# Half-precision operand pairs in the down projection of both feed-forward layers

## The chip, the cores and the metric

The kernel runs on one core of a Trainium2 chip. Its engines work from queues of their own, each strictly in order: TensorE (PE; its weight loads are PEld), VectorE (DVE), ScalarE (ACT), GpSimd (POOL) and the sync engine (SP), which issues most loads. The metric is device time in microseconds for one execution: the median of several runs. One more execution is recorded by the hardware profiler.

## The reference

Two layers of a diffusion backbone run over 1024 latent tokens and 256 context tokens of width 1024. After each mixer comes a modulated SwiGLU feed-forward layer of inner width 2816:

```python
def swiglu(u, w_gate, w_up, w_down):
    return (jax.nn.silu(u @ w_gate) * (u @ w_up)) @ w_down
...
h_lat = h_lat + g2 * swiglu(modulate(rms_norm(h_lat, norm2_g[i]), sh2, sc2),
                            ffn_w_gate[i], ffn_w_up[i], ffn_w_down[i])
if not last:
    h_ctx = h_ctx + cg1 * y_ctx
    h_ctx = h_ctx + cg2 * swiglu(modulate(rms_norm(h_ctx, norm2_g[i]), csh2, csc2),
                                 ffn_w_gate[i], ffn_w_up[i], ffn_w_down[i])
```

All inputs and outputs are float32.

## The kernel before

Activations are held with features on the 128 partitions and tokens along the free axis. The inner width is 22 blocks of 128, worked on as 11 pairs (`n2`); the latent tokens are two halves of 512 columns. A pair of blocks times the two halves is a 2x2 block product, and it is done by Winograd's scheme: seven products in place of eight, each of sums and differences of the blocks.

Float32 precision comes from operand pairs: each operand is split into a high and a low part, and every product takes three matmuls (high by high, high by low, low by high). There are two kinds of split. `split` casts to F32R on ScalarE and subtracts on VectorE. `half_split` scales by a column, rounds to float16 on ScalarE, and forms the scaled rest in float16 on VectorE. Gate and up use scaled half-precision pairs, down uses F32R pairs.

**Gate and up** (`ffn`). For each pair i the weights of gate, then up, are loaded (`wino_weights`), bounded by `weight_scale` (a scale from the sum of absolute values, so that no scaled weight can overflow), and split into seven operand pairs. `wino_steps` then issues the products in steps: A11 with B11 into PSUM tile `pa`; A12 with B21 into `pc`; S1 with T1 into `pb`; then S2, S3 and A22 onto `pa`, with a copy taken between them (`snap`); last S4 with B22 onto `pb`. Each product is 12 matmuls (four blocks of the contraction by three), each of 512 columns. The steps of gate and up of pair i are mixed with the last steps of up of pair i - 1. PSUM tiles come from `PS`, by turns out of one pool of six and one of two banks (out of the six alone in layer 0 at this point). `finish(i)` multiplies the four evicted up blocks by the gate blocks (after SiLU), forms the sums and differences that down needs, and stores seven tiles to DRAM (`bops`). The gate tiles come from a pool of four. `sums(i)` loads the four blocks of pair i of the down weights, forms S1 to S4 on VectorE, and stores them to DRAM (`sops`). In layer 0, the conditioning of the next layer (`ada_group`, line 448) is computed on VectorE meanwhile.

The instructions of each engine are put in order by a scheduler at build time, which goes by dependencies, buffers and the order of the program; tiles of a pool are given out in the program's order.

**Down** (`down`). Seven products, each summed over the 11 pairs: for every pair the operand of weights and that of activations are loaded side by side into one tile of 128x1024, split, and multiplied with 12 matmuls into four PSUM tiles (three for each tile). Tiles come from a pool of 20. `evict` scales a finished block by a column of the conditioning and adds it to the residual stream. In the last product the last three pairs (layer 0) or four pairs (layer 1) are multiplied block by block at the end; in layer 1 in two halves of 256 columns. The context tokens' down in layer 0 is a separate loop at the end of `down`.

Of the kernel before, what the change touches and what calls it, by code (L numbers as in the profile page):

```python
# [10 lines left out]
F32 = mybir.dt.float32  # L11
F32R = mybir.dt.float32r
# [17 lines left out]
WID = {0: 512, 1: 512, 2: 256, 3: 256, 4: 256}  # L30
OFF = {0: 0, 1: 512, 3: 512, 4: 768}
KSTART = (0, 8, 24, 32)
PAD_C, PAD_T, SHIFT = 96, 112, 16
BOPS = ("B11", "B21", "T2", "T1", "T3", "B22", "T4")


# [165 lines left out]
class Builder:  # L202
# [970 lines left out]
        self.ucol = cols  # L1173
        self.usi = us[:, 1:2]

    def weight_scale(self, tiles):

        nc = self.nc
        n = len(tiles)
        st = self.pt.tile([P, 16], F32, tag="st", name=self.nm("st"))  # L1180
        junk = self.T(BF16, 1024)
        for k, t in enumerate(tiles):
            nc.scalar.activation(junk[:, :t.shape[1]], t, AF.Abs, scale=2.0 ** -15, accum_out=st[:, k:k + 1])
        sb = st[:, 8:9].bitcast(BF16)
        with nc.allow_low_precision(reason="a bound, within a factor of two"):
            nc.vector.tensor_reduce(sb[:, 0:1], st[:, :n], axis=AX, op=ADD)
        ps = self.PS()
        self.mm(ps[:, 0:1], self.ones.bitcast(BF16)[:, 1::2], sb[:, 0:1], True, True)
        k = 3 * len(self.wsc)
        s, b, inv = (self.wcol[:, k + j:k + j + 1] for j in range(3))  # L1190
        nc.vector.tensor_scalar(b, ps[:, 0:1], 1e-30, None, op0=MAX)
        nc.vector.reciprocal(s, b)
        nc.vector.tensor_scalar(inv, b, self.usi, None, op0=MUL)
        return s, inv
# [178 lines left out]
    def ffn(self, l, u, h, hs, second, after, keep=None, begun={}):  # L1373
# [3 lines left out]
        bops = [{k: self.DR([P, 512]) for k in BOPS} for _ in range(n2)]  # L1377
        sops = [{k: self.DR([P, 512]) for k in ("S1", "S2", "S3", "S4")} for _ in range(n2)]
        hidc = [self.DR([P, 2, 256]) for _ in range(n2 if u is not None else 0)]
        def sums(i):  # L1380

            w = a["down"][l]
            t = [self.S2() for _ in range(4)]
            a21, a22, a11, a12 = t
            with self.follow(self.last_ld):
                for x, (k, r) in zip(t, ((0, 1), (1, 1), (0, 0), (1, 0))):
                    self.ld(x, w[2 * i + k, r])
            nc.vector.tensor_tensor(a22, a21, a22, ADD)  # L1388
# [28 lines left out]
        def finish(i, gate):  # L1417

            up = self.res
            inv = self.wsc[(l, i, 1)][1]  # L1420
            for k, g in gate.items():
                nc.vector.scalar_tensor_tensor(g, up[k], inv, g, op0=MUL, op1=MUL)  # L1422
            b11, b12, b21, b22 = gate[(0, 1)], gate[(0, 0)], gate[(1, 1)], gate[(1, 0)]
            t1, t2, t4 = up[(0, 0)], up[(0, 1)], up[(1, 1)]
            nc.vector.tensor_tensor(t1, b12, b11, SUB)
# [17 lines left out]
        for i in range(n2):  # L1443
            g, up = begun.get((i, 0)), begun.get((i, 1))
            if g is None or not g.whole:
                wg = waiting.pop((i, 0))
                w = next(wg)
                next(wg)
            fetch(i, 1)
            if g is None:  # L1450
                g = Steps(self.wino_steps(w, self.G))
                g.to(1)
            if prev is not None:
                prev[0].to(7)
                finish(i - 1, prev[1])
            wu = waiting.pop((i, 1))
            w = next(wu)
            if up is None:
                up = Steps(self.wino_steps(w, self.TK))
            if i == 0:  # L1460
                for k, _ in enumerate(second):
                    if k == 11:
                        next(wu)
            next(wu, None)
            fetch(i + 1, 0)
            for k in (3, 4, 5) if i == 0 and l == 1 else ():
# [12 lines left out]
            up.to(5)  # L1479
            prev = (up, gate)  # L1480
            for k in (2 * i - 2, 2 * i - 1) if l == 1 else (9, 10) if i == 9 else (i,) if i < 9 else ():
                if 0 <= k < n2:
                    sums(k)
            for _ in range(2):
                next(todo, None)
        prev[0].to(7)
        finish(n2 - 1, prev[1])
        self.down(l, bops, sops, hidc, hs, h, todo, after, keep)

    def down(self, l, bops, sops, hidc, hs, h, todo, after, keep):
        nc, a = self.nc, self.a
        w = a["down"][l]
        n2 = NFB // 2
        self.banks = 6

        def operands(asrc, bsrc, own):
            hi, lo = self.S4(F32R), self.S4(F32R)
            f = self.S4() if own else lo.bitcast(F32)  # L1500
            self.ld(f[:, :512], asrc)
            self.ld(f[:, 512:], bsrc)
            self.split(f, hi, lo)
            return hi, lo

        def prods(acc, ops, j, c0, c1, first, last):
# [20 lines left out]
        def evict(acc, r, j, pc, final):  # L1527
            nb = 4 * r + j
            n = WID[pc]
            c0 = OFF[pc] % 512 if pc > 2 else 0  # L1530
            t = h.ap(0, nb, pc)
            nc.vector.scalar_tensor_tensor(t, acc[j][:, c0:c0 + n], self.ada_col(l, pc, 5, nb), t, op0=MUL, op1=ADD)
            if final and pc < 3:
                self.square(t, nb, pc)
                if l == 0 and pc < 2:
                    self.lda(keep[nb][:, pc * 512:pc * 512 + 512], t)
            elif final and j < 3:
                x = self.TK()
# [15 lines left out]
        for p, (ak, bk, r, pc, final) in enumerate(seq):  # L1554
            acc = sets[p % 2]
            late = []
            for i in range(n2):
# [700 lines left out]
```

## Time and profile before

| | us |
|---|---|
| runs, median of 3 (lowest to highest) | 3015.81 (3011.55 to 3017.45) |
| profiled execution, its own time | 3016.71 |
| profiled execution, span from first to last instruction | 3014.9 |
| mean granted TensorE clock | 0.982 |

The page sums up the engines' busy time over the span and lists groups of instructions by source line. These are the largest groups of matmuls; the columns after the bar are the busy time, the mean duration in ns, and the idle time of the engine before them with what ended it:

```profile
L1324 PE MATMUL ps<-s,s 128*128 128x512 f16 x2100 | 477.3, 383 | 16.5 <-DVE s L1221 8.6
L1511 PE MATMUL ps<-s,s 128*128 128x512 f32 (+1 forms) x1000 | 261.2, 384 | 9.0 <-DVE s L289 8.7
```

Line 1324 is gate and up, line 1511 is down, lines 287 and 289 are the two steps of `split`, lines 1146 and 1147 those of `half_split`, and lines 1183 to 1193 are `weight_scale`. Matmuls overlap, so that their rate is read from how many fit into a stretch, not from the duration of one. Rows of a stretch show the stretch's length, then busy time and count by engine, the granted clock (PEclk), the share of the DMA engines, and GB/s.

### The profile page before, as it was taken

The numbers are of one execution on the slowest core, as the hardware profiler recorded it, in microseconds if no ns is written. First come the engines' busy times: TensorE is split into PE (matmuls) and PEld (weight loads), VectorE is DVE, ScalarE is ACT, GpSimd is POOL, SyncE is SP. The second block draws the span as 40 slices with busy tenths as digits, with TensorE's granted clock in tenths as the row PEclk, the third lists the DMA queues.
The fourth block names the chain that finished last, engine by engine and source line by source line (L and its number), as shares of the span: only waits on it lengthen the run. The fifth ranks groups of instructions, "written<-read, shape, count | busy, mean of one in ns | idle before, by whom it ended". The sixth has DMA issues, their size and how long they took to land. (4 is left out here: it accounts for less than half of the span.)

```text
span 3014.9 us, 46087 instructions
## 1 busy us (share of the span) xinstructions
PE 2864.5 (95%) x16364; PEld 2085.2 (69%) x16364; DVE 2108.4 (70%) x4181; ACT 1511.8 (50%) x2761; POOL 530.8 (18%) x883
## 2 busy tenths in 40 slices
PE   7899999899998999999999999999999799999997
PEld 3678888888897444447778888878777344444886
DVE  5767786674677988866767437777776898765555
ACT  4663325452456555443445336777774655543433
POOL 1012013451111212131020002222231022112000
PEclk9899999999999999999999999999999899999999
DMA  7564545366555555657874344444555376424663
GB/s 256 190 202 166 176 143 173 119 189 213 200 210 196 211 187 206 221 207 270 290 245 153 126 130 119 134 137 121 180 175 192 134 275 235 149 81 165 217 192 130
DMA packets 253681, 551.47 MB, mean 183 GB/s; under 512 B 33926, under 2 KB 69448, under 8 KB 253450
## 3 DMA queue, kind: packets, MB, share of 16 engines
q1 hardware_dynamic: 191658, 357.63, 35.7%
q0 software_dynamic: 59488, 186.70, 17.5%
q10 hardware_dynamic: 2304, 4.20, 0.4%
q8 instruction: 129, 2.11, 0.3%
q14 instruction: 102, 0.84, 0.1%
HBM read 420.20 MB, written 119.80 MB: 179 GB/s over the span
## 5 line engine op out<-in xcount | busy, mean ns | idle before, releaser
L1324 PE MATMUL ps<-s,s 128*128 128x512 f16 x2100 | 477.3, 383 | 16.5 <-DVE s L1221 8.6
L1324 PEld LDWEIGHTS <-s 128*128 128x128 f16 x2640 | 259.1, 98 | 334.5 <-issue 28.4
L283 PE MATMUL ps<-s,wh 128*128 128x256 f32 (+1 forms) x1780 | 393.6, 327 | 1.5 <-ACT wh L287 1.5
L283 PEld LDWEIGHTS ps<-s,wh 128*128 128x128 f32 x1780 | 293.2, 188 | 36.5 <-ACT wh L287 3.1
L283 PE MATMUL pq<-s,wh 128*128 128x512 f32 (+1 forms) x972 | 297.4, 385 | 4.7 <-DVE s L2088 2.5
L1511 PE MATMUL ps<-s,s 128*128 128x512 f32 (+1 forms) x1000 | 261.2, 384 | 9.0 <-DVE s L289 8.7
L287 ACT CAST s<-s 128x1024 fp32r<-128x1024 f32 (+2 forms) x188 | 171.7, 942 | 180.0 <-DMA s<-d 146.9
L283 PE MATMUL ps<-s,wl 128*128 128x256 f32 (+1 forms) x890 | 257.7, 327 | 2.3 <-DVE wl L289 2.3
L283 PE MATMUL ps<-s,s 128*128 128x64 f16 (+3 forms) x2663 | 216.1, 233 | 24.0 <-DVE st L1800 9.9
L287 ACT CAST wh<-ws 128x1024 fp32r<-128x1024 f32 (+1 forms) x99 | 100.4, 1014 | 265.5 <-PE ps L283 163.8
L289 DVE TENSOR_TENSOR s<-s,s 128x1024 fp32r<-128x1024 f32 (+2 forms) x166 | 190.8, 1182 | 45.7 <-ACT s L287 44.8
L1511 PEld LDWEIGHTS ps<-s,s 128*128 128x128 f32 x1000 | 183.8, 188 | 50.3 <-DVE s L289 14.1
L289 DVE TENSOR_TENSOR wl<-ws,wh 128x1024 fp32r<-128x1024 f32 (+1 forms) x99 | 116.6, 1178 | 128.3 <-ACT wh L287 123.7
L283 PEld LDWEIGHTS pq<-s,wh 128*128 128x128 f32 x972 | 176.3, 191 | 39.4 <-DVE s L2088 2.7
L1324 PE MATMUL ps<-s,wh 128*128 128x512 f16 x624 | 190.9, 386 | 3.1 <-ACT wh L1146 2.1
L283 PE MATMUL ps<-s,mat 128*128 128x512 f32 x684 | 177.2, 405 | 6.8 <-DVE s L289 4.0
L283 PE MATMUL pq<-s,wl 128*128 128x512 f32 (+1 forms) x486 | 180.8, 381 | 0.1
L335 ACT CAST mat<-cs 128x1024 fp32r<-128x1024 f16 (+2 forms) x120 | 111.7, 935 | 132.1 <-PE ps L283 38.0
L283 PEld LDWEIGHTS ps<-s,wl 128*128 128x128 f32 x890 | 163.2, 188 | 20.3 <-DVE wl L289 3.7
L274 POOL DMA_DIRECT2D d<-s x153 | 82.7, 541 | 521.3 <-DVE s L1388 224.3
L283 PEld LDWEIGHTS ps<-s,mat 128*128 128x128 f32 x684 | 130.6, 194 | 42.0 <-DVE s L289 6.8
L1511 PE MATMUL ps<-s 128*128 128x512 f32 (+1 forms) x500 | 152.4, 387 | 1.1 <-ACT s L287 1.0
(393 smaller groups left out, 5825.4 us busy)
## 6 DMA issues: line engine op xcount, KB each, us to landing
s<-d SPq DMA_DIRECT2D x286, 256.0 KB, 3.7
s<-in_down SPq DMA_DIRECT2D x154, 256.0 KB, 4.6
d<-s POOLq DMA_DIRECT2D x137, 256.0 KB, 2.5
d<-tk POOLq DMA_DIRECT2D x98, 256.0 KB, 3.3
s<-in_ada_w POOLq DMA_DIRECT2D x48, 512.0 KB, 4.4
g<-in_bias POOLq DMA_DIRECT2D x128, 192.0 KB, 3.2
s<-in_up SPq DMA_DIRECT2D x46, 512.0 KB, 3.5
s<-in_gate SPq DMA_DIRECT2D x44, 512.0 KB, 4.1
```

What stands on the lines that cost most here:

```text
L274: self.last_ldr = self.nc.gpsimd.dma_start(out, in_).ins
L283: self.nc.tensor.matmul(o, l, r, start=st, stop=sp)
L287: self.last_hi = nc.scalar.copy(hi, src).ins
L289: self.last_lo = eng.tensor_tensor(lo, src, hi.bitcast(F32), SUB).ins
L335: self.nc.scalar.copy(m, st)
L1324: nc.tensor.matmul(ps, x[:, sl], y, start=first and j == 0 and x is wh and y is xh, stop=j == 3 and x is wl, skip_group_check=True)
L1511: m = nc.tensor.matmul(acc[j][:, c0:c1], x[:, sl], y[:, xs], start=first and k == 0, stop=last and k == 2, skip_group_check=True)
```

## The change

Down uses scaled half-precision pairs for all pairs of blocks but the last one, in both layers.

- `abs_bound` is the first part of `weight_scale`, made a function of its own: absolute sums of the given tiles on ScalarE (`activation` with `Abs` and an accumulated column), their sum on VectorE, and a one-column matmul with ones that adds it up over the partitions into a new PSUM tile.
- `sums(i)` bounds its four tiles and keeps the running maximum `wmax`. In layer 1 `sums` runs one pair earlier than before: 2i - 1 and 2i in place of 2i - 2 and 2i - 1.
- `finish(0)` bounds the four products, makes `ratio` from that bound and `wmax` and scales the four tiles by it on ScalarE; in the following pairs `ratio` is part of the scale that was applied anyway. `finish(1)` to `finish(9)` bound their four products and keep the running maximum `hmax`. `finish(10)` makes no bound.
- `down` makes one factor `sw` from the two running maxima. The operands of pairs 0 to 9 are loaded into a tile of their own and split by `half_split` into one float16 tile that holds both parts; those of pair 10 stay F32R, with the weights scaled by `sw` squared. `evict` takes the scale back out with the column `gcol`, the conditioning times `inv`.
- The first padding tile is narrower by the 32 columns that the new columns take.

```diff
-    def weight_scale(self, tiles):
+    def abs_bound(self, tiles):
...
         ps = self.PS()
         self.mm(ps[:, 0:1], self.ones.bitcast(BF16)[:, 1::2], sb[:, 0:1], True, True)
+        return ps[:, 0:1]
...
@@ ffn, sums
             with self.follow(self.last_ld):
                 for x, (k, r) in zip(t, ((0, 1), (1, 1), (0, 0), (1, 0))):
                     self.ld(x, w[2 * i + k, r])
+            nc.vector.tensor_scalar(wmax, self.abs_bound(t), wmax, None, op0=MAX)
             nc.vector.tensor_tensor(a22, a21, a22, ADD)
...
@@ ffn, finish
-            inv = self.wsc[(l, i, 1)][1]
+            scale = self.wsc[(l, i, 1)][1]
+            if i:
+                nc.vector.tensor_tensor(inv, scale, ratio, MUL)
+                scale = inv
             for k, g in gate.items():
-                nc.vector.scalar_tensor_tensor(g, up[k], inv, g, op0=MUL, op1=MUL)
+                nc.vector.scalar_tensor_tensor(g, up[k], scale, g, op0=MUL, op1=MUL)
+            if i == 0:
+                b = self.abs_bound(list(gate.values()))
+                nc.vector.tensor_scalar(ratio, b, 1e-30, None, op0=MAX)
+                nc.vector.reciprocal(ratio, ratio)
+                nc.vector.tensor_scalar(ratio, ratio, wmax, 2.0 ** 60, op0=MUL, op1=MIN)
+                nc.vector.tensor_scalar(hmax, b, ratio, hmax, op0=MUL, op1=MAX)
+                for g in gate.values():
+                    nc.scalar.mul(g, g, ratio)
+            elif i < n2 - 1:
+                nc.vector.tensor_scalar(hmax, self.abs_bound(list(gate.values())), hmax, None, op0=MAX)
...
-            for k in (2 * i - 2, 2 * i - 1) if l == 1 else (9, 10) if i == 9 else (i,) if i < 9 else ():
+            for k in (2 * i - 1, 2 * i) if l == 1 else (9, 10) if i == 9 else (i,) if i < 9 else ():
...
@@ down
+        nc.vector.tensor_tensor(big, wmax, hmax, MAX)
+        nc.vector.reciprocal(sw, big)
+        nc.vector.tensor_tensor(sw2, sw, sw, MUL)
+        nc.vector.reciprocal(inv, ratio)
+        nc.vector.tensor_scalar(inv, inv, big, big, op0=MUL, op1=MUL)
+        gcol = self.C(8)
+        nc.vector.tensor_scalar(gcol, self.ada[(l, 0)][:, 40:48], inv, None, op0=MUL)
 
-        def operands(asrc, bsrc, own):
-            hi, lo = self.S4(F32R), self.S4(F32R)
-            f = self.S4() if own else lo.bitcast(F32)
+        def operands(asrc, bsrc, last):
+            f = self.S4()
             self.ld(f[:, :512], asrc)
             self.ld(f[:, 512:], bsrc)
-            self.split(f, hi, lo)
+            if last:
+                hi, lo = self.S4(F32R), self.S4(F32R)
+                nc.scalar.activation(hi[:, :512], f[:, :512], AF.Copy, scale=sw2)
+                nc.scalar.copy(hi[:, 512:], f[:, 512:])
+                nc.vector.scalar_tensor_tensor(lo[:, :512], f[:, :512], sw2, hi[:, :512].bitcast(F32), op0=MUL, op1=SUB)
+                nc.vector.tensor_tensor(lo[:, 512:], f[:, 512:], hi[:, 512:].bitcast(F32), SUB)
+            else:
+                t = self.S4(F16, 2048)
+                hi, lo = t[:, :1024], t[:, 1024:]
+                self.half_split(f, sw, hi, lo)
             return hi, lo
...
-            nc.vector.scalar_tensor_tensor(t, acc[j][:, c0:c0 + n], self.ada_col(l, pc, 5, nb), t, op0=MUL, op1=ADD)
+            nc.vector.scalar_tensor_tensor(t, acc[j][:, c0:c0 + n], gcol[:, nb:nb + 1], t, op0=MUL, op1=ADD)
...
-                ops = operands(src, bops[i][bk], ak in raw)
+                ops = operands(src, bops[i][bk], i == n2 - 1)
```

More of the change, by code (lines that the diff above doesn't have):

```diff
@@ L32 @@
 KSTART = (0, 8, 24, 32)
-PAD_C, PAD_T, SHIFT = 96, 112, 16
+PAD_C, PAD_T, SHIFT = 64, 112, 16
 BOPS = ("B11", "B21", "T2", "T1", "T3", "B22", "T4")
@@ L1188, in weight_scale @@
         self.mm(ps[:, 0:1], self.ones.bitcast(BF16)[:, 1::2], sb[:, 0:1], True, True)
+        return ps[:, 0:1]
+    def weight_scale(self, tiles):
+        nc = self.nc
+        ps = self.abs_bound(tiles)
         k = 3 * len(self.wsc)
         s, b, inv = (self.wcol[:, k + j:k + j + 1] for j in range(3))
-        nc.vector.tensor_scalar(b, ps[:, 0:1], 1e-30, None, op0=MAX)
+        nc.vector.tensor_scalar(b, ps, 1e-30, None, op0=MAX)
         nc.vector.reciprocal(s, b)
@@ L1379, in ffn @@
         hidc = [self.DR([P, 2, 256]) for _ in range(n2 if u is not None else 0)]
+        dc = self.C(8)
+        nc.vector.memset(dc, 1e-30)
+        wmax, hmax, ratio, inv = (dc[:, k:k + 1] for k in range(4))
         def sums(i):
@@ L1487, in ffn, with down @@
         finish(n2 - 1, prev[1])
-        self.down(l, bops, sops, hidc, hs, h, todo, after, keep)
-    def down(self, l, bops, sops, hidc, hs, h, todo, after, keep):
+        self.down(l, bops, sops, hidc, hs, h, todo, after, keep, dc)
+    def down(self, l, bops, sops, hidc, hs, h, todo, after, keep, dc):
         nc, a = self.nc, self.a
@@ L1496, in down @@
         self.banks = 6
-        def operands(asrc, bsrc, own):
-            hi, lo = self.S4(F32R), self.S4(F32R)
-            f = self.S4() if own else lo.bitcast(F32)
+        wmax, hmax, ratio, inv, big, sw, sw2 = (dc[:, k:k + 1] for k in range(7))
+        nc.vector.tensor_tensor(big, wmax, hmax, MAX)
[7 more added lines that the diff above has]
+            f = self.S4()
             self.ld(f[:, :512], asrc)
             self.ld(f[:, 512:], bsrc)
-            self.split(f, hi, lo)
+            if last:
[8 more added lines that the diff above has]
+                self.half_split(f, sw, hi, lo)
             return hi, lo
```

## The prediction

> **What bounds the kernel now.** I read the page first, then the stretches of the two feed-forward layers, then single lines inside them.
>
> ```profile
> span 3014.9 us, 46087 instructions
> PE 2864.5 (95%) x16364; PEld 2085.2 (69%) x16364; DVE 2108.4 (70%) x4181; ACT 1511.8 (50%) x2761; POOL 530.8 (18%) x883
> ```
>
> ```profile
> core 0: us, PE busy (x) PEld busy (x) DVE busy (x) ACT busy (x) POOL busy (x), PEclk, DMA share, GB/s
> 965.00:1359.00 394.00, 387.45 (x1794) 174.85 (x1794) 329.43 (x687) 199.62 (x316) 81.96 (x153) 0.99 0.58 206
> 2410.00:2500.00 90.00, 88.34 (x413) 39.75 (x412) 82.60 (x146) 50.44 (x83) 21.58 (x40) 1.00 0.74 271
> 2500.00:2740.00 240.00, 237.25 (x1104) 107.30 (x1103) 168.87 (x290) 121.33 (x192) 44.63 (x83) 0.99 0.43 159
> 2783.00:2850.00 67.00, 67.00 (x297) 55.09 (x296) 33.65 (x36) 25.00 (x27) 3.18 (x6) 1.00 0.68 225
> ```
>
> Gate and up of layer 0 fill 965 to 1359, down follows; layer 1 has gate and up to 2783, down after it. TensorE is busy for 98% of gate and up, so what it waits for there is added to the end. VectorE is close behind in layer 0: 329 of 394 us.
>
> Two stretches without a wait give the price of one matmul, the first of half-precision operands (line 1324), the second of F32R (line 1511):
>
> ```profile
> 2515.00:2735.00 220.00, 220.00 (x1020) 98.77 (x1019) 1.00 0.42 156
> 2790.00:2960.00 170.00, 170.00 (x752) 140.77 (x751) 1.00 0.62 198
> ```
>
> 220/1019 is 215.9 ns and 170/751 is 226.4 ns from start to start: F32R costs 10.5 ns more.
>
> **Down: what is removed.** The last of eleven pairs stays F32R. Of 924 down matmuls in layer 0, 840 become half precision; of 972 in layer 1 (four pairs of its last product go in halves), 876, 72 of them half as wide. Counted by width that is 840 + 804 + 36 = 1680, by 10.5 ns: **-17.6 us**. It needs the operands to stay hidden:
>
> ```profile
> L289 DVE TENSOR_TENSOR s<-s,s 128x1024 fp32r<-128x1024 f32 x69 | 80.7, 1220 | 16.0 <-ACT s L287 15.9
> L287 ACT CAST s<-s 128x1024 fp32r<-128x1024 f32 x69 | 70.2, 1049 | 69.8 <-DMA s<-d 57.9 <-DVE tk L1353 4.5 <-PE pq L1511 4.4
> L1146 ACT ACTIVATE wh<-ws,c 128x1024 f16<-128x1024 f32 x21 | 24.1, 1147 | 14.7 <-DVE c L1192 8.5 <-PE ps L1324 6.2
> L1147 DVE SCALAR_TENSOR_TENSOR wl<-ws,c,wh 128x1024 f16<-128x1024 f32 x21 | 26.9, 1282 | 11.8 <-ACT wh L1146 11.8
> ```
>
> One operand feeds 12 matmuls, 2.59 us. Its two steps grow from 1.05 + 1.22 to 1.15 + 1.28 us on two engines, each under half of that, so I cost them at nothing; without the cover it would be 0.16 us by 140 operands, 22 us. TensorE's waits in down of layer 0 are
>
> ```profile
> PE ps L1511 <- DVE s L289: 7.8, 8, 1.8
> PE ps L1511 <- ACT s L287: 1.0, 1, 1.0
> ```
>
> 8.8 us. An operand now holds one buffer while it waits instead of two, which lets loads run ahead; the faster stretch asks for 5% more bytes a second. I bound this by -8.8 and +8.8 and take 0. The scale columns at the start of down (seven operations on 128x1) rest on a bound made a pair earlier.
>
> **The bounds: what is added.** Each layer gets 21 more bounds: one per pair of down weights (in `sums`), one for the products of each of pairs 0 to 9 (in `finish`). A bound is four absolute sums on ScalarE, a reduction on VectorE, a one-column matmul, a read of it on VectorE. Here is what the matmul itself costs and what it does when its reduction is late:
>
> ```profile
> 957.42 0.16 PE L283 MATMUL ps<-st,c 128*128 128x1 bf16 x1 [0.16 <-DVE st L1186]
> 965.96 0.16 PE L283 MATMUL ps<-st,c 128*128 128x1 bf16 x1 [8.37 <-DVE st L1186]
> 965.99 1.01 PE L1324 MATMUL ps<-s,wh 128*128 128x512 f16 x2
> ```
>
> Ready, it holds the queue for 0.03 us: 42 of them are 1.3 us. Late, the whole of TensorE stands behind it, here for 8.37 us. So the question is where the new ones stand. In `sums` (22) they stand behind loads that run far ahead. In layer 0, pair 4, the subtractions behind those loads ran 50 us before the add of pair 4's last product:
>
> ```profile
> 1107.14 0.68 DVE L1388 TENSOR_TENSOR s<-s,s 128x512 f32<-128x512 f32 x1
> 1158.66 0.69 DVE L1353 TENSOR_TENSOR tk<-ps,tk 128x512 f32<-128x512 f32 x1 [0.71 <-PE ps L1324]
> ```
>
> and the new matmul stands 48 matmuls (10 us) before that add's product ends. I cost these at nothing, and at 0 to 10 us where layer 1 starts, since there they now come a pair earlier; I take 0. The 20 in `finish` are another matter. This is the built order of the changed kernel on TensorE, layer 0, pair 4 (U, G: up and gate products, 12 matmuls each):
>
> ```
> U4 S2 | bound sums(4) | bound weights up(5) | G5 A11 | U4 S3 | U4 A22 | U4 S4 |
> bound finish(4) | bound weights gate(6) | G5 A12 | G5 S1 | G5 S2 ...
> ```
>
> PSUM tiles are given out in program order, and the bound's tile precedes those of G5 A12 and S1, so these can't move ahead, as they do in the kernel before. The bound of finish(4) needs U4 S4 evicted, multiplied by the gate, summed on ScalarE and reduced, and TensorE has nothing else meanwhile. The prices on VectorE, from start to start, stand in one crowded stretch of its timeline; two more rows give ScalarE's sum, two the ends of a matmul and a copy:
>
> ```profile
> 1159.88 0.69 DVE L448 CUSTOM_DVE_ANT_0 s<-s,s 128x512 f32<-128x512 f32 x1
> 1160.49 0.75 DVE L1422 SCALAR_TENSOR_TENSOR g<-tk,c,g 128x512 f32<-128x512 f32 x1
> 1161.15 0.15 DVE L450 TENSOR_TENSOR c<-ah 128x1 f32<-128x1 f32 x1
> 1161.23 0.69 DVE L448 CUSTOM_DVE_ANT_0 s<-s,s 128x512 f32<-128x512 f32 x1
> ...
> 1163.11 0.16 DVE L1186 TENSOR_REDUCE st<-st 128x1 bf16<-128x2 f32 x1 [0.58 <-ACT t L1183]
> 1163.18 0.68 DVE L448 CUSTOM_DVE_ANT_0 t<-s,s 128x512 f32<-128x512 f32 x1
> 1163.79 0.08 DVE L448 DVE_READ_ACCUMULATOR2_ANT ah<- 128x1 f32 x1
> 1163.79 0.69 DVE L1425 TENSOR_TENSOR tk<-g,g 128x512 f32<-128x512 f32 x1
> 1164.39 0.15 DVE L450 TENSOR_TENSOR c<-ah 128x1 f32<-128x1 f32 x1
> ```
>
> ```profile
> 2313.38 0.62 ACT L1183 ACTIVATE t<-g 128x512 bf16<-128x512 f32 x1
> 2313.90 0.19 ACT L1183 ACTIVATION_READ_ACCUMULATOR t<-g 128x1 f32 x1
> 2314.12 0.63 ACT L1183 ACTIVATE t<-g 128x512 bf16<-128x512 f32 x1
> ```
>
> ```profile
> L1324 PE MATMUL pq<-s,s x540: 379/379/390, 2408.5 to 2781.5; 128*128 128x512 f16 x180
> L1329 ACT COPY tk<-ps 128x512 f32<-128x512 f32 x31 | 18.0, 581 | 27.1 <-PE ps L1324 13.3 <-PE ps L283 8.1 <-DVE c L1191 4.6
> ```
>
> An add of 512 columns takes 0.60 (1163.79 to 1164.39), a gate multiplication 0.66, a conditioning product with its read 0.61, a small one or a reduction 0.07, an absolute sum 0.75.
>
> Pair 4, zero at the start of the last matmul of U4 S3. It ends at 0.38, its copy on ScalarE at 0.96, and VectorE adds to that. From this add to the one behind U4 S4 its queue holds 18 operations: six adds (3.6), two gate multiplications (1.3), three conditioning products (1.8), four small ones (0.3) and the three reads inside the products: 7.0, so that add starts at 8.0, though U4 S4 ended at 5.6 (24 by 0.216 + 0.38). Then that add, two others, a small one and the last gate multiplication: 2.5. Then ScalarE sums that tile and two queued behind it (3 by 0.75 = 2.25), while VectorE has four adds and a small one ahead of the reduction, 2.5, the longer. With the reduction (0.15 to its end) the bound is ready at 13.2. TensorE ran dry at 5.4 (25 by 0.216): it waits **7.8 us**. Hand-overs between engines are left out, which can only lengthen it.
>
> Counted the same way, pairs 0 to 9 of layer 0 wait 5.7, 8.2, 7.9, 8.9, 7.8, 8.9, 9.4, 9.0, 7.5, 4.0: 77 us. In layer 1 the order puts 13 to 44 matmuls (2.8 to 9.5 us) in between: 1.9, 1.1, 1.5, 6.0, 2.3, 0, 0.1, 3.9, 0, 0: 17 us. **Waits: +94 us.** Two lower ends: counted from the end of S4, with VectorE up to date by then, 55 + 17 = 72 us; with the bound's own steps alone (0.38 + 0.69 + 0.75 + 2.25 + 0.15 = 4.2, less what stands in between), 32 + 2 = 34 us. Above, 40 us more if the sums' loads or ScalarE are late too. I take 94: VectorE is the fuller queue, and in the row
>
> ```profile
> L1353 DVE TENSOR_TENSOR tk<-ps,tk 128x512 f32<-128x512 f32 x10 | 6.9, 686 | 2.5 <-PE ps L1324 2.5
> ```
>
> only 2.5 us of waiting for TensorE stand before ten such adds: it is behind TensorE there already.
>
> **The clock after a wait.** The stretches right behind two waits, the one of 8.37 us and one that the timeline gives as
>
> ```profile
> 1228.15 1.02 PE L1324 MATMUL ps<-s,s 128*128 128x512 f16 x4 [2.09 <-DVE g L1353]
> ```
>
> show the granted clock (third number from the right):
>
> ```profile
> 966.00:969.60 3.60, 3.60 (x10) 1.30 (x10) 2.93 (x12) 1.46 (x3) 0.00 (x0) 0.50 0.58 203
> 969.60:975.00 5.40, 5.40 (x27) 2.45 (x26) 5.40 (x16) 3.72 (x7) 0.00 (x0) 1.00 0.37 108
> 1229.00:1232.40 3.40, 3.40 (x10) 1.19 (x9) 3.07 (x9) 1.68 (x3) 1.11 (x3) 0.51 0.20 82
> ```
>
> Half speed for 3.6 us loses 1.8. Ten waits of layer 0 and three of layer 1 are over 2.09 us: 13 by 1.8, **+23 us**; the lower end is none. [...]
>
> **The rest.** Pair 0's products are scaled by four more ScalarE steps before they are stored, under 4 us by the rows above; TensorE has 48 matmuls (10 us) behind that bound: nothing. TensorE's old waits in layer 0's gate and up (394.00 - 387.45) fall inside the new ones: -6.5, or 0.
>
> **Sum**, against the profiled execution's own 3016.71 us (span 3014.9; the median of the runs is 3015.81, 0.9 lower): 3016.7 - 17.6 + 1.3 + 94 + 23 - 6.5 = 3111, with hand-overs **3115**.
>
> **Rivals.**
> 1. VectorE has worked off its queue when a pair's last product ends: waits of 72 us, sum 3089. For it: after the first wait VectorE gets time to catch up. Against it: its operations are tied to the same pair's products. 22%.
> 2. Only the bound's own steps are waited for: 34 us, and the clock falls in layer 0 alone (18): 3016.7 - 17.6 + 1.3 + 34 + 18 - 6.5 = 3046. For it: much of VectorE's queue there has its inputs early. Against it: the queue is in order. 10%.
> 3. The other side: the bound is covered everywhere, as the order does for pairs 8 and 9 of layer 1 (9 us of matmuls ahead of it). It decides from a cover of about 10 us a pair; then -17.6 + 1.3 and perhaps the 8.8 of down: 2992, faster than before. Against it: in layer 0 six pairs have no matmul in between. 4%.
> 4. ScalarE with eight more sums a pair, or `sums` at the start of layer 1, is late on top of the forecast: the 40 us above, 3155. For it: VectorE's 329 of 394 us leave little to catch up with. 12%.
> 5. Down doesn't gain (operands late, as the 8.8 us of waits show it can be): 3133, inside the forecast's own range and counted with it.
>
> **How the numbers follow.** Forecast 52% (own range 3090 to 3140), rivals 22, 10, 4 and 12. The range 3055 to 3165 leaves out rival 3, most of rival 2 and a third of rival 4, under 2 in 10. A change within 0.2% can't be told from none here. Slower by more: all but rival 3, 0.95; faster 0.04; same 0.01.
>
> **What would show it.** In the changed kernel's waits of TensorE, the reduction of the bound (line 1186) should end some 80 us of idling in layer 0 and 20 in layer 1, in about 17 waits of 1 to 10 us, each in front of the one-column matmul that follows a pair's last product; gate and up of layer 0 should take near 480 us instead of 394; half-clock stretches should stand behind the waits; and down should run at 216 ns a matmul except its last pair. Waits of 4 us and less in layer 0 would make rival 2 right; TensorE as full as before in gate and up would make the forecast wrong altogether.

## The result and the profile after

The changed kernel takes 3176.68 us (median of 4 runs, 3174.02 to 3181.63) against 3016.63 us for the kernel before: ratio 1.0535, 95% interval 1.0517 to 1.0554. It is slower, as forecast, but 62 us above the forecast of 3115 and 12 above the range.

From the page of the changed kernel, the span and the share of each engine; the instructions grew by 488, TensorE by 42 matmuls:

```profile
span 3173.8 us, 46575 instructions
...
PE 2886.5 (91%) x16406; PEld 1951.8 (61%) x16406; DVE 2138.5 (67%) x4319; ACT 1645.6 (52%) x3117; POOL 530.0 (17%) x883
```

TensorE is busy for 22 us more and idle for 137 us more. The stages, cut at the starts of the first and last matmul of the gate-and-up line and of the down line (idle counts gaps of over 0.1 us between matmuls):

| stage | before, us | after, us | difference | idle of TensorE |
|---|---|---|---|---|
| gate and up, layer 0 | 410.4 | 538.3 | +127.9 | 5.6 to 106.8 |
| to the last down matmul, layer 0 | 224.2 | 206.3 | -17.9 | 9.0 to 3.2 |
| between the layers | 744.1 | 751.2 | +7.1 | |
| gate and up, layer 1 | 439.4 | 483.7 | +44.3 | 24.8 to 61.1 |
| to the last down matmul, layer 1 | 212.6 | 202.7 | -9.9 | 1.0 to 0.0 |
| ahead of layer 0's pairs, and behind the last | | | +7.4 | |

The sum is 158.9 us, the difference of the two spans. The stretches outside the layers run the same code in both; in the profiles below the one between the layers took 741 to 754 us, so those +14 are not followed up.

Windows of the changed kernel (start:end and length, then busy time of TensorE, weight loads, VectorE, ScalarE and POOL with instructions, granted clock, DMA share, GB/s): gate and up of layers 0 and 1, and a stretch of each down. They answer to the first rows of windows in the prediction.

```profile
970.50:1509.00 538.50, 431.70 (x1896) 188.97 (x1896) 353.14 (x770) 271.30 (x499) 83.38 (x155) 0.90 0.46 161
2466.00:2950.00 484.00, 422.89 (x1902) 187.67 (x1902) 323.59 (x602) 280.72 (x529) 71.99 (x134) 0.94 0.42 153
...
1520.00:1700.00 180.00, 180.00 (x834) 87.64 (x832) 133.48 (x236) 84.32 (x101) 23.60 (x45) 1.00 0.82 290
2960.00:3140.00 180.00, 180.00 (x835) 87.65 (x834) 105.84 (x111) 84.10 (x91) 0.00 (x0) 1.00 0.54 193
```

The same two stages before:

```profile
966.00:1376.40 410.40, 404.81 (x1875) 183.14 (x1875) 338.80 (x703) 205.55 (x323) 84.06 (x156) 0.99 0.58 205
2344.70:2784.00 439.30, 414.52 (x1888) 185.82 (x1888) 324.25 (x550) 226.31 (x361) 73.24 (x136) 0.97 0.46 169
```

Down runs without a gap at 180/834, 215.8 ns a matmul with some of the last pair among them, which is the half-precision price of the prediction. In gate and up, ScalarE has 66 and 54 us more work, VectorE 14 and nothing; TensorE works 27 and 8 us longer on about the same matmuls, which is the slower clock (0.90 against 0.99, and 0.94 against 0.97). The rest is idleness. The waits of TensorE in layer 0 (who waits, for which engine, tile and line; us, times, longest):

```profile
PE ps L283 <- DVE st L1186: 58.2, 7, 10.5
PE ps L1330 <- ACT g L1335: 36.4, 5, 10.7
PE ps L1330 <- ACT tk L1335: 16.0, 8, 3.0
PE ps L1330 <- DVE tk L1354: 4.6, 4, 1.4
```

The first row holds the old wait of 8.37 us and six of the ten new big ones, 49.8 us. The four others, of pairs 1, 3, 5 and 8, stand in the second row, 36.1 us: they don't end with a reduction but with the copy of a gate product on ScalarE. Big waits by pair, 0 to 9: 8.68, 8.33, 9.04, 9.34, 8.88, 7.72, 10.45, 8.47, 10.72, 4.29, 86 us. The last two rows are 20.6 us of a second kind, which the forecast doesn't have.

Pair 4, which the prediction worked through, in the timeline (start, length, engine and line; in brackets the idle time ahead and what ended it):

```profile
1202.02 2.75 PE L1330 MATMUL ps<-s,s 128*128 128x512 f16 x12
...
1204.86 0.56 ACT L1335 COPY tk<-ps 128x512 f32<-128x512 f32 x1
...
1205.47 2.75 PE L1330 MATMUL ps<-s,s 128*128 128x512 f16 x12 [0.70 <-ACT tk L1335]
...
1208.88 0.69 DVE L1354 TENSOR_TENSOR tk<-ps,tk 128x512 f32<-128x512 f32 x1
...
1209.62 2.75 PE L1330 MATMUL ps<-s,s 128*128 128x512 f16 x12 [1.40 <-DVE tk L1354]
...
1215.92 0.69 DVE L1359 TENSOR_TENSOR tk<-ps,tk 128x512 f32<-128x512 f32 x1
...
1217.79 0.75 DVE L1436 SCALAR_TENSOR_TENSOR g<-tk,c,g 128x512 f32<-128x512 f32 x1
...
1218.57 0.63 ACT L1183 ACTIVATE t<-g 128x512 bf16<-128x512 f32 x1 [7.24 <-DVE g L1436]
...
1221.05 0.15 DVE L1186 TENSOR_REDUCE st<-st 128x1 bf16<-128x4 f32 x1
...
1221.25 0.19 PE L283 MATMUL ps<-st,c 128*128 128x1 bf16 x2 [8.88 <-DVE st L1186]
```

The three blocks of 12 are U4 S3, A22 and S4, with nothing else between them. The chain is the predicted one, link by link, to the one-column matmul at 1221.25 (the row counts it together with the matmul of the next weights' bound). But it begins late: VectorE starts the add that reads S3's copy 3.5 us after that copy's end (1208.88 against 1205.42), and S4 waits 1.40 us for that add, which reads the PSUM tile that S4 adds to. Then 6.4 us of VectorE's queue stand ahead of S4's own add: 1215.92, when S4 had ended at 1212.37.

In pairs 3, 5, 7 and 8 the first of these small waits is longer. Timeline behind pair 5's S3:

```profile
1255.28 1.04 ACT L1183 ACTIVATE t<-ws 128x1024 bf16<-128x1024 f32 x1
...
1257.54 0.56 ACT L1335 COPY tk<-ps 128x512 f32<-128x512 f32 x1
...
1258.15 2.29 PE L1330 MATMUL ps<-s,s 128*128 128x512 f16 x5 [2.98 <-ACT tk L1335]
```

S3's copy stands on ScalarE behind the weights' steps, and TensorE, with no other product to turn to, waits 2.98 us.

And pair 3. In the four pairs 1, 3, 5 and 8 the built order has matmuls between the last product and the bound, 9 to 12 of G S2 in the trace, which the prediction took for cover:

```profile
1169.54 0.63 ACT L1183 ACTIVATE t<-g 128x512 bf16<-128x512 f32 x1
...
1170.95 0.59 ACT L1335 COPY g<-ps 128x512 f32<-128x512 f32 x1 [0.69 <-DMA d<-g]
...
1171.59 2.72 PE L1330 MATMUL ps<-s,s 128*128 128x512 f16 x6 [9.34 <-ACT g L1335]
```

These matmuls themselves wait for the copy of G4 A11, which stands behind the pair's own absolute sums on ScalarE and needs a buffer that the store of an older product has to free. They are no cover.

### The profile page after: what moved, and what is told of

It reads as the page before. It is cut to its first block, busy times and chain, and to the rows that moved or that the text cites. A ratio compares the mean times of both kernels' runs of the same rounds, so it can differ in the third digit from the quotient of the medians.

```text
span 3173.8 us, 46575 instructions
## 1 busy us (share of the span) xinstructions
PE 2886.5 (91%) x16406; PEld 1951.8 (61%) x16406; DVE 2138.5 (67%) x4319; ACT 1645.6 (52%) x3117; POOL 530.0 (17%) x883
## 5 line engine op out<-in xcount | busy, mean ns | idle before, releaser
L1330 PE MATMUL ps<-s,s 128*128 128x512 f16 x2316 | 537.9, 389 | 72.7 <-ACT g L1335 48.6
L1330 PEld LDWEIGHTS <-s 128*128 128x128 f16 x2640 | 262.9, 100 | 410.5 <-issue 116.7
L1552 PE MATMUL ps<-s 128*128 128x512 f16 (+2 forms) x1404 | 315.9, 376 | 2.4 <-DVE s L1147 2.4
L1552 PEld LDWEIGHTS <-s 128*128 128x128 f16 x1716 | 166.1, 98 | 198.6 <-issue 7.0
L1146 ACT ACTIVATE s<-s,c 128x1024 f16<-128x1024 f32 (+1 forms) x183 | 188.6, 1041 | 103.8 <-DMA s<-d 67.9
L1147 DVE SCALAR_TENSOR_TENSOR s<-s,c,s 128x1024 f16<-128x1024 f32 (+1 forms) x183 | 207.2, 1155 | 21.6 <-ACT s L1146 21.5
L1330 PE MATMUL ps<-s,wh 128*128 128x512 f16 x616 | 199.5, 405 | 3.0 <-ACT wh L1146 3.0
L1330 PEld LDWEIGHTS <-wh 128*128 128x128 f16 x704 | 69.4, 102 | 132.4 <-issue 37.6
```

What stands on the lines that cost most here:

```text
L1146: nc.scalar.activation(hi, src, AF.Copy, scale=scale)
L1147: nc.vector.scalar_tensor_tensor(lo, src, scale, hi, op0=MUL, op1=SUB)
L1330: nc.tensor.matmul(ps, x[:, sl], y, start=first and j == 0 and x is wh and y is xh, stop=j == 3 and x is wl, skip_group_check=True)
L1552: m = nc.tensor.matmul(acc[j][:, c0:c1], x[:, sl], y[:, xs], start=first and k == 0, stop=last and k == 2, skip_group_check=True)
```

## The experiments

Medians of 4 to 10 runs; each ratio is to the kernel before, run on the same chip. Lines are added or removed against the changed kernel unless another is named. In the profiles of the twenty kernels, one execution each, the stretch ahead of layer 0's pairs took 964 to 976 us and the one between the layers 741 to 754 us, with the same code: a difference of a few us between two kernels can't by itself be put down to the edit.

**Which bounds cost, and does down gain?** Three kernels leave out one kind of bound, the other, or both.

```diff
 # no finish bounds
+        nc.vector.memset(hmax, 0.2)
+        nc.vector.memset(ratio, 2.0 ** -10)
-            if i == 0:
-                b = self.abs_bound(list(gate.values()))
-...
-                nc.vector.tensor_scalar(hmax, self.abs_bound(list(gate.values())), hmax, None, op0=MAX)
 # no sums bounds
+        nc.vector.memset(wmax, 0.13)
-            nc.vector.tensor_scalar(wmax, self.abs_bound(t), wmax, None, op0=MAX)
 # no bounds: both
```

> Leaves out the bounds of the products (in finish): ratio and hmax are constants, so the operands are scaled by a factor that no longer bounds them by the data. The bounds of down's weights (in sums) stay. Theory P (place: the one-column matmul of finish holds TensorE's in-order queue until the pair's products are multiplied, summed and reduced): the ten big waits of layer 0 (8 to 11 us each) and their half-clock stretches go, gate and up of layer 0 falls from 538 to 425 us or less, the whole to about 3025 (3010 to 3040). Theory S (the bounds in sums cost most, by their absolute sums on ScalarE ahead of up's copies): still 3100 or more.

> Leaves out the bounds of down's weights (in sums): wmax is a constant. The bounds of the products stay. Theory P: the big waits stay, only the small second waits before up's products (some 20 us in layer 0, less in layer 1) and the seam at the start of layer 1 go: 3145 (3130 to 3160). Theory S: 3080 or less.

> Leaves out both kinds of bounds, constants in their place: down alone is changed, to scaled half-precision operands. If the wait is all that the change costs: the time before less down's 28 us (18 and 10 us in the two layers), 2990 (2983 to 2998). If half-precision operands cost something of their own elsewhere: 3000 or more.

Measured: without finish's bounds 2992.4 us (0.9913, 0.9894 to 0.9933); without those of sums 3162.5 (1.0478, 1.0455 to 1.0500); without both 2985.8 (0.9889, 0.9868 to 0.9911). The first came out 18 us under its range, the second 2 us above, the third inside. So down in half precision is worth 30 us, the weights' bounds by themselves cost 6.6 us (2992.4 - 2985.8), and the products' bounds by themselves 177 (3162.5 - 2985.8). In windows of the kernel without bounds, gate and up of layer 0 are within 2 us of before (410.4), and layer 1's down runs without a gap, as in the changed kernel (44 of the window's matmuls have half the width):

```profile
965.70:1377.90 412.20, 403.39 (x1874) 182.17 (x1874) 344.60 (x727) 211.08 (x328) 83.87 (x155) 1.00 0.61 212
...
2775.00:2960.00 185.00, 185.00 (x877) 92.16 (x876) 105.81 (x114) 81.27 (x88) 3.25 (x6) 1.00 0.54 180
```

The small waits in layer 0 without the bounds of sums, and without those of finish:

```profile
PE ps L1330 <- ACT tk L1335: 20.5, 9, 3.0
```

```profile
PE ps L1330 <- ACT tk L1335: 1.3, 2, 1.0
```

They stay when only the weights' bounds go, and nearly go with the products' bounds. So they don't come from the sums of down's weights, which the second expectation had blamed.

**Place or load?** Two kernels do all the work and issue the end of finish's bound (for pairs 1 to 9) behind the next pair's gate products; in the second the reduction stays in finish. A third needs no matmul for those pairs.

```diff
 # late place; "matmul late" has the reduction in abs_sums
-                nc.vector.tensor_scalar(hmax, self.abs_bound(list(gate.values())), hmax, None, op0=MAX)
+                late.append(self.abs_sums(list(gate.values())))
...
             g.to(7)
+            while late:
+                nc.vector.tensor_scalar(hmax, self.bound_end(late.pop(), 4), hmax, None, op0=MAX)
 # running columns (for sums(1) and later too)
+                st = self.abs_sums(tiles)
+                nc.vector.tensor_tensor(run[:, k:k + 4], run[:, k:k + 4], st[:, :4], MAX)
```

> Computes all that the changed kernel computes, with as many instructions on every engine; only the reduction, the one-column matmul and its read for the products of pairs 1 to 9 are issued later, behind the next pair's gate products. Theory P (place): 3040 (3025 to 3060), since only pair 0's wait and those of sums are left. Theory L (load: four more absolute sums a pair on ScalarE and the work on VectorE make these engines late wherever the matmul stands): 3120 or more.

> As the late place, but the reduction on VectorE stays in finish and only the one-column matmul and its read are issued behind the next pair's gate products. Place theory: the later place still waited 2.5 to 4.5 us a pair because the reduction had moved too and stood behind that pair's adds on VectorE; with the reduction early the waits in pairs 1 to 9 of layer 0 go, 3025 (3010 to 3040). Load theory: 3060 or more.

> All absolute sums stay on ScalarE; for all pairs but the first they go into running maxima, a column for each of four tiles, by one small VectorE operation, and TensorE adds these up once at the end of the pairs instead of once a pair (the sum of the largest is never under the largest sum, so the bound holds). Place theory: 3005 (2997 to 3015), which is the kernel without bounds, 2986, and pair 0's wait with its slow clock (8.7 + 3 us in layer 0, some 3 in layer 1) and a few us for the sums. Load theory (the 75 us that the later place kept above the kernel without the products' bounds are ScalarE's and VectorE's additional work): 3045 or more.

Measured: late place 3067.8 (1.0167, 1.0141 to 1.0192), matmul late 3072.2 (1.0179, 1.0163 to 1.0196), running columns 3052.4 (1.0108, 1.0093 to 1.0123). The place is worth 109 us of 191, with the same work on every engine; without the matmul it is 124. But all three came out above the place theory's ranges, the second and third within the load theory's, and where the reduction stands makes no clear difference (3067.8 and 3072.2). In the first two the moved matmuls of layer 0 stand without a wait, and the small waits are gone (2.3 and 2.5 us for copies of `tk`), so that these too came with the place. What is left there besides the old wait and pair 0's is 20 us before reductions of two columns, which are the bounds of gate and up weights. The running columns show the same; their waits in layer 0, and the timeline of one of them:

```profile
PE ps L283 <- DVE st L1194: 38.3, 10, 8.7
```

```profile
1094.91 1.04 ACT L1186 ACTIVATE t<-ws 128x1024 bf16<-128x1024 f32 x1
...
1097.79 1.04 ACT L1186 ACTIVATE t<-s 128x1024 bf16<-128x1024 f32 x1
...
1099.98 0.15 DVE L1194 TENSOR_REDUCE st<-st 128x1 bf16<-128x2 f32 x1
...
1100.19 0.16 PE L283 MATMUL ps<-st,c 128*128 128x1 bf16 x1 [2.49 <-DVE st L1194]
```

It sums `ws`, not a product: this is the bound of the next gate weights, which the kernel before makes too. Its two sums share ScalarE with four more a pair, and its matmul now stands right behind a pair's last product, with nothing between; in the kernel before it ran without a wait in these pairs. Six pairs in a row wait 2.49 us there.

**Is VectorE's queue part of the wait?**

```diff
+            if where == "s4" and nb < 22:
+                for c in conds:
+                    nc.vector.tensor_copy(self.ada[(l, c)][:, nb:nb + 1], self.adab[:, nb:nb + 1])
+                yield
+                continue
```

> The changed kernel with 22 blocks of layer 1's conditioning left out (the products that VectorE makes during the pairs of layer 0; a copy of one column stands in for each, so layer 1 computes with other factors). Tests the step that counts VectorE's queue into the wait. As forecast (three products, 1.8 us, and their small operations stand ahead of pair 4's add in VectorE's queue): nine waits of layer 0 shorter by some 2 us each, 3155 (3140 to 3162). Rival 1 (VectorE has worked off its queue when the pair's last product ends): no shorter, 3170 to 3182.

Measured: 3162.0 (1.0471, 1.0453 to 1.0488), 15 us less, at the upper edge of the forecast. In layer 0 the big waits of pairs 2 to 7 fall from 7.7-10.5 to 5.6-6.8 us; those of pairs 1 and 8 don't (9.83 and 11.23), and a small one of 2.99 stands in each of pairs 3 to 8. VectorE's queue is in the wait, as the forecast had it and rival 1 did not; pair 4's timeline above says the same, where the queue held S4's add back for 3.5 us after S4's end.

**What the late weights' bound costs.** Two kernels take pair 0's wait out of the running columns (pair 0 stored unscaled, in F32R through down) without and with layer 1's sums in their old places; four move the next gate weights' fetch.

```diff
 # pair 0 late, against the running columns
-                b = self.abs_bound(list(gate.values()))
-...
+                late.append(self.abs_sums(list(gate.values())))
-                ops = operands(src, bops[i][bk], i == n2 - 1)
+                ops = operands(src, bops[i][bk], sw3 if i == 0 else sw2 if i == n2 - 1 else None)
 # fetch moved: ahead of finish / behind g.to(5) (S2) / behind g.to(7) (all gate products)
-            next(wu, None)
-            fetch(i + 1, 0)
+            next(wu, None)
...
+            fetch(i + 1, 0)
```

> As the running columns, and pair 0 is stored unscaled and goes through down in F32R as the last pair does, so that its bound, which gives the ratio, can be issued behind pair 1's gate products. Place theory: pair 0's wait gets cover, 84 matmuls a layer go back to F32R (2 by 0.9 us): 8 to 12 us under the running columns, 2995 (2988 to 3004). Load theory: as the running columns, within 3 us.

> The same with the weights' bound where the changed kernel has it. If that bound is what costs in all pairs of layer 0: 25 us or more above the two others, 3025 to 3045. If the old places of the sums are what was missing: within 5 us of them.

> The running columns, with the next gate weights' loads and their bound issued ahead of finish instead of behind it: their two absolute sums then stand ahead of the four of finish on ScalarE, and their one-column matmul ahead of the pair's last products on TensorE. Theory W (the 60 us that the running columns keep above the kernel without the products' bounds are the weights' own bounds, made late by the four sums on ScalarE, each holding TensorE 2.49 us and then a slow clock): 3010 (2998 to 3025). Theory L (ScalarE or VectorE are simply full, wherever that bound stands): 3045 or more.

> The running columns, with the next gate weights' loads and their bound issued later, behind this pair's gate products up to S2: their one-column matmul then has 36 matmuls or more (7.8 us) behind the pair's last product as cover. Theory W: 3005 (2995 to 3020). Theory L: 3045 or more. If the loads of these weights come too late by it, TensorE waits on ws or wh at the start of a pair instead.

> As the kernel before this, one step later still: behind all of this pair's gate products. Theory W: within 8 us of that kernel, as both have cover enough. Theory L: 3045 or more. Weights too late: above that kernel by 10 us or more, with waits on ws or wh.

> The next gate weights' bound behind S2, and pair 0 unscaled with its bound issued late, as in the kernel that did so alone. Theory W: pair 0's first wait (8.7 us in layer 0, with its slow clock) had only been passed on to a weights' bound there; now it goes, 8 to 12 us under the kernel with the bound behind S2 alone, 2995 (2985 to 3008). Theory L: 3045 or more.

| kernel | us | ratio (interval) |
|---|---|---|
| pair 0 late | 3050.6 | 1.0107 (1.0091 to 1.0122) |
| pair 0 late, old sums | 3049.3 | 1.0104 (1.0089 to 1.0119) |
| fetch ahead of finish | 3029.7 | 1.0035 (1.0020 to 1.0049) |
| fetch behind S2 | 3053.9 | 1.0116 (1.0096 to 1.0136) |
| fetch behind the gate products | 3026.7 | 1.0034 (1.0020 to 1.0048) |
| fetch behind S2, pair 0 late | 3066.6 | 1.0155 (1.0124 to 1.0185) |

Pair 0 alone gains 2 us at most, where 8 to 12 were expected: its wait goes, and the weights' bounds of the pairs behind it take it over (8.25 and 7.11 us). Layer 1's sums in their old places change 1 us. Moving the weights' bound ahead or far behind is worth 23 and 26 us. Both times lie below theory L's, but the first is 5 us above theory W's range, and some 40 us above the kernel without bounds are left: the weights' bounds are 23 to 26 us of the 60 that theory W gave them. Fetch behind the gate products, waits in layer 0:

```profile
PE ps L283 <- DVE st L1194: 16.9, 3, 8.4
PE ps L1338 <- ACT g L1343: 9.9, 5, 2.8
```

Of ten waits for a reduction three are left: the old one, pair 0's and one of 0.91 us. Fetch behind S2 missed by 50 us and is no faster than the running columns, and the fetch behind the gate products, expected within 8 us of it, is 27 us faster. The weights' reductions are gone from layer 0 there too, but copies of gate products on ScalarE take their place:

```profile
PE ps L1338 <- ACT g L1343: 16.4, 8, 4.4
PE ps L283 <- DVE st L1194: 16.2, 2, 8.4
```

From the first gate product to the last down matmul layer 0 is still 13 us shorter than in the running columns (652.5 against 665.1 us), but layer 1 is 8 us longer (659.7 against 652.1), and the stretches ahead of and between the layers are 13 us longer. Why this middle place is worse than both others, and worse still with pair 0 late, was not settled; the move changes the order of much else.

**Inside the wait or on top of it? And the rest.** The same move on the changed kernel itself; then both remedies, with the fetch late, early, or early in layer 0 and late in layer 1; and the move alone on the kernel before.

```diff
 # the changed kernel, and the kernel before
-            fetch(i + 1, 0)
...
             g.to(7)
+            fetch(i + 1, 0)
 # mixed
+            if l == 0:
+                fetch(i + 1, 0)
             if prev is not None:
...
             g.to(7)
+            if l == 1:
+                fetch(i + 1, 0)
```

> The changed kernel with all its bounds, each with its matmul; only the next gate weights' loads and bound are moved behind this pair's gate products, so that TensorE meets the bound of finish alone between a pair's last product and the next pair's. If the weights' bound adds to the wait: 3115 to 3150, nearer 3115 if the 60 us that the running columns kept add in full. If it lies inside the wait for the products' bound (both wait for ScalarE at the same place): 3165 to 3185.

> Running columns, the weights' bound behind the gate products, pair 0 unscaled with its bound and the ratio at the end of pair 1, and layer 1's sums in their old places (none in its first pair). If the 41 us are pair 0 and the start of layer 1: 3000 (2992 to 3010), below the kernel before. If they are ScalarE's load in all pairs: 3018 or more.

> The same, with the weights' bound ahead of finish instead of behind the gate products. Pair 0 and start of layer 1: 3003 (2993 to 3012). Load: 3020 or more.

> Running columns, pair 0 unscaled and late, layer 1's sums in their old places; the next gate weights' fetch ahead of finish in layer 0 and behind the gate products in layer 1. If the two places add up: 3007 (3000 to 3013). If they don't (what one layer gains the seam between them gives back): 3012 to 3018.

> The kernel before, F32R in down and no new bounds, with only the next gate weights' fetch moved behind the gate products. If the move is worth something by itself: 3000 to 3010. If it only undoes what the sums had spoilt: 3015 to 3030.

| kernel | us | ratio (interval) |
|---|---|---|
| changed, fetch behind the gate products | 3167.6 | 1.0499 (1.0479 to 1.0519) |
| running columns, pair 0 late, fetch late | 3013.3 | 0.9986 (0.9975 to 0.9997) |
| the same, fetch early | 3016.2 | 0.9995 (0.9982 to 1.0007) |
| the same, early in layer 0, late in layer 1 | 3005.4 | 0.9958 (0.9943 to 0.9974) |
| before, fetch behind the gate products | 3009.0 | 0.9974 (0.9964 to 0.9984) |

On the changed kernel the move gains 9 us only, 7 of them in the profiles ahead of layer 0, so there the weights' bound lies inside the wait for the products' bound. On the running columns it is bare. With both remedies and the fetch in one place the two kernels came out between their theories (3013 and 3016), the weights' bound in its old place 33 us or more above them: pair 0's wait, which gained almost nothing alone, gains 13 us once that bound is away (with layer 1's sums moved back as well). The mixed kernel, with every bound, is faster than the kernel before by 0.42%. That isn't all down's doing: moving the fetch behind the gate products gains 8 us by itself on the kernel before, so that 3.6 us are left, and the two ratios' intervals overlap. That half-precision down with all its bounds gains anything over F32R with such a move is not shown. In the best kernel gate and up of layer 0 are still 427 us long:

```profile
967.10:1393.80 426.70, 413.85 (x1900) 186.38 (x1900) 344.30 (x749) 262.90 (x496) 84.31 (x156) 0.99 0.56 201
```

with 12.9 us of idleness. It keeps 20 us above the kernel without bounds (3005.4 - 2985.8), and the trace shows no single wait that they go to.

## Why the prediction came out short

- **What bounds the kernel, and the mechanism.** Right in the main: TensorE idles once a pair behind the chain named, and moving that matmul away, with all work kept, gives back 109 us. But only six of layer 0's ten big waits stand in front of finish's one-column matmul, as foretold, with 50 us of the 80; the four others, 36 us, stand in front of gate products whose copy is behind the same absolute sums on ScalarE.
- **Down: -17.6, with -8.8 to +8.8 for its waits.** The matmul price was right (215.8 ns). Most of the waits went too: idleness in the two stretches fell by 6.8 us (9.0 to 3.2 and 1.0 to 0.0). By stage the whole is -17.9 and -9.9, near the lower end of the bound that was taken at 0.
- **"Waits: +94".** The step that failed, in size: it gave the waits 50 us too little. With the -6.5 for old waits the sum has 87.5 us; idleness grew by 101.2 in layer 0 (106.8 - 5.6) and 36.3 in layer 1 (61.1 - 24.8): 137.5. Three things in it:
  1. Layer 0's small waits, 20.6 us that the sum has at nothing. The count for pair 4 set its zero at S3 and let A22 and S4 run through at 0.216 us a matmul, with VectorE up to date when S3's copy was ready. Here VectorE was 3.5 us behind, and A22 and S4 themselves waited 0.70 and 1.40 us. Idle in pair 4: 10.98 us against 7.8.
  2. Layer 0's big waits: 86 us against 77. The matmuls taken for cover in pairs 1, 3, 5 and 8 covered nothing, but these four make little of the difference (36.1 us against 33.5); in the six others the chain was longer than counted.
  3. Layer 1's count of 17 us was half of the 36.3 that came. Its waits for reductions are 24 us, those for gate copies 18. Of the 24, 7.7 stand in the first 15 us of the layer, ahead of any finish, where the kernel before waits about as long for other things; the other 17 and the 18 are the forecast's own kind, 35 us. The matmuls in between covered less than counted, because they wait for gate copies themselves. After, and before:

```profile
PE pq L283 <- DVE st L1186: 12.5, 3, 5.9
PE ps L1330 <- ACT g L1335: 12.2, 4, 4.9
PE ps L283 <- DVE st L1186: 11.9, 2, 6.9
...
PE pq L1330 <- ACT g L1335: 5.7, 1, 5.7
```

```profile
PE ps L1324 <- ACT g L1329: 2.7, 1, 2.7
...
PE pq L283 <- DVE st L1186: 0.9, 1, 0.9
...
PE ps L283 <- DVE st L1186: 0.5, 2, 0.3
```

- **The clock, +23.** 35 came by the windows (26.9 + 8.4 us more busy time), with the 1.3 us of the new matmuls in it. In windows laid on the half-clock stretches, layer 0's ten big waits lose 21.4 us, 2.1 each where 1.8 was counted; the small waits of pairs 3 and 5, which were not among the 13 counted, lose 4.3; and layer 1 lost 9.4 us more than before where 5.4 was counted. The 1.8 is no fixed price: the last section has a wait of 2.91 us that was followed by full clock.
- **"Sums" at nothing.** 6.6 us by themselves (14 on top of the products' bounds, 3176.7 - 3162.5), so nothing was somewhat too low. The bound of 0 to 10 was set for the start of layer 1; by the profiles of the kernels without the products' bounds the 6.6 lie in layer 0 (gate and up 419.9 us with the sums, 412.3 without).
- **Rivals.** Rival 1 (VectorE caught up) falls by the kernel without layer 1's conditioning: shorter by 15 us with 2 us a pair less in the queue. Rivals 2 and 3 fall with the sizes. Rival 4 (ScalarE late on top) named a real load but not where it would act: in the changed kernel moving the weights' bound away gives 9 us, and the load shows in full, some 60 us (3052.4 - 2992.4, pair 0's bound included), only once the matmul is out of the way. Rival 5 falls: down gains.

Summed by stage terms: 137.5 idle, 35 clock, -28 down, 14 outside: 159 us for a forecast of 98. The waits were 50 us too small, the clock 12, the 14 outside were not forecast, and down gained 10 more; less the 4 for hand-overs and the 1.3 for the matmuls, which the sum held apart, that is the 61 us by which the forecast was short. The 14 outside are in the range by which these stretches differ between kernels, so no cause is claimed for them.

## What to carry to other kernels

A tiny instruction on an in-order queue can cost all of the chain that it waits for, here 4.29 to 10.45 us for one of 0.16: before adding one, ask what stands between its inputs and its place, and whether what you count as cover is itself waiting on the same engines. A running bound can be kept per partition beside the matrix work and added up once; that took 124 us off here. When a wait is removed, look what was lying inside it: here the weights' bound was bare next, and only with both moved, and pair 0's as well, did the kernel come under the one before. And try the moves on the old kernel too: most of that last gain was the fetch's, not half precision's.

## What the runs showed of the hardware

How long TensorE stood idle did not alone decide its clock. In the running columns a wait of 2.49 us, from 1097.70 to 1100.19, was followed by a granted clock of 0.59 in the next 3.40 us and of 0.91 in the 3.40 us after them (TensorE's busy time stands behind the length, the clock is third from the right):

```profile
1097.70:1100.20 2.50, 0.01 (x1) 0.01 (x1) 2.50 (x6) 1.22 (x3) 0.00 (x0) 1.00 0.90 310
1100.20:1103.60 3.40, 3.40 (x11) 1.36 (x11) 3.40 (x9) 2.83 (x9) 1.10 (x3) 0.59 1.05 412
1103.60:1107.00 3.40, 3.40 (x16) 1.43 (x15) 3.40 (x13) 3.31 (x8) 0.52 (x1) 0.91 0.58 233
```

In the kernel with the fetch behind S2 a longer one, 2.91 us from 1107.07 to 1109.98, was followed by full clock:

```profile
1107.10:1110.00 2.90, 0.02 (x1) 0.02 (x1) 2.90 (x6) 2.90 (x7) 0.54 (x1) 1.00 0.93 307
1110.00:1113.40 3.40, 3.40 (x17) 1.56 (x17) 3.40 (x10) 1.28 (x3) 0.00 (x0) 1.00 1.02 279
```

The wait of 2.09 us in the prediction, shorter than both, has 0.51 behind it. So these three waits don't stand in the order of their lengths; what else decides the clock behind a wait was not shown.
